# A whole-bank output norm in a hand-written order, other boundaries, and another spread of the conditioning products

## The chip, the cores and the metric

The kernel runs on one core of one Trainium2 chip. The metric is the time of one execution on the device, in microseconds. A core has a matrix engine (PE; its weight loads, PEld, run beside its products), a vector engine (DVE), a scalar engine (ACT), POOL, and SP, which here only issues loads. PE writes into PSUM banks of 128 x 512 floats, which DVE and ACT read.

## The reference

Two layers of a decoder trunk over 256 tokens of width 1024. Each layer has three sublayers, a half-step SwiGLU, a mixer and another half-step SwiGLU: six in all, named ffn0, hg, ffn1, ffn2, gm, ffn3 here. Each sublayer normalises before and after, and takes a shift, a scale and a gate from a vector c:

```python
def sublayer(x, fn, pre_g, post_g, shift, scale, gate, res_w):
    h = rms_norm(x, pre_g) * (1.0 + scale) + shift
    return x + res_w * gate * rms_norm(fn(h), post_g)
...
mod = (cond @ ada_w[i] + ada_b[i])
```

The first mixer is HGRN2, a gated linear recurrence of 8 heads, whose output is normalised per head and token over 128 values, multiplied by a silu gate, and projected:

```python
o = rms_norm(o, out_norm) * gate
return o.reshape(B, S, D_MODEL).astype(h.dtype) @ w_out
```

The second mixer is a gMLP: gelu, a layer norm of one half, a causal mixing over tokens, a product with the other half, a projection.

## The kernel before, in words

The 256 tokens are two tiles (t = 0, 1) of 128. x stays in SBUF through all six sublayers, so time goes from sublayer to sublayer and all else is prefetched.

**Weights.** They come in blocks of two halves. For a half, `cast` (L113) has SP load 512 KB into a buffer `raw` and ACT round it to the high part (L122); `sub` (L129) has DVE take the low part, raw minus high (L132). `halves(n)` does both for n halves. A product of activations and weights is three matmuls, high x high, high x low, low x high (`mm3`, L162 to L164). `next_block` hands out a block that is ready and prepares some ahead.

**Conditioning products.** `cond @ ada_w` is cut into 144 products over a 128 x 1024 tile, each a 512 KB load (`ada`) by SP and one DVE instruction with its reading of the sum (L192). Some are made when shift and scale of the next sublayer (`pre_cols`) or the gate (`gate_tile`) need them; the others are spread between the weight blocks: `pace(upto, blocks)` (L154) says that by the end of so many blocks the products up to `upto` are to be made. The table `bgs` in `run` gives `upto` for each sublayer. The load goes on the same SP queue as the weights, and its tile must have been freed by DVE.

**Order.** A scheduler places most instructions; the order that the program is written in counts there, with a few added "after" edges (`self.gate`, `self.hold`). From `boundary` (L297) to `close` (L371) the order of ACT, DVE and PE is as written: a `manual_schedule` region.

**A boundary**, between two sublayers, computes the last output matmuls `mm(t, h)` for each tile and each half h of 512 columns; squares the halves (ACT, `square`, L235); multiplies by the gate (DVE, `gated`, L310); scales the sum and adds it to x in two halves (`residual`, L255); squares x; scales it to `xn` (`scaled`, L293 DVE and L295 ACT); transposes it on PE into `npa` (L271); and makes the next sublayer's input, its high part on ACT (`h_high`, L274), then a full copy `hf` on DVE (L284) and the low part on DVE (L287), both in `h_low`. `half_mean` (L242) makes the bias `be` of the second half's sqrt. In between stands `p0`, the first matmuls of the next sublayer over t = 0 (`pps`, L412): 30 of them, then npa of (1,0), 6, npa of (1,1), and the rest. `halves(4)` and `halves(2)` at the start, one half block around the second residual, and one before `p0`, keep the weights coming: 8 in all.

**The HGRN** (`hgrn`, L627) makes its projections in `feat` and `tok`, and its attention in `attn(hb)` for two blocks of four heads. `attn` goes through seven levels of chunk size h (64, 32, 16, 8, 4, 2, 1): DVE makes differences and products (L724, L729, L735), ACT an exponential (L80), PE scores into `ab` (L741), DVE copies them under a mask (L712). Each level is a chain DVE, ACT, DVE, PE, DVE. `zip_steps` deals one step of projection to each step of attention, so that PE has work: attn(0) is mixed with `feat` and `tok`, attn(1) with the last `tok` and with `outs`, which holds the norm of the first four heads and their 48 output matmuls. At the end PE forms the outputs of four heads in two PSUM banks, `ops` (L774, L776).

`finish(hb, ops)` (L781) is the output norm. ACT squares each of the eight 128 x 128 pieces with an accumulated sum (L787); `r8` is the inverse root of the mean, for hb = 0 by Newton steps on DVE (`rsqrt`, L84 to L101), for hb = 1 by ACT's sqrt and a reciprocal (L792); DVE multiplies each piece by r8 and the gate `gg` in one instruction out of PSUM (L800); PE transposes four of them into a bank `ots` (L805); ACT and DVE split that into high and low part (L809, L810), the stationary operands of the output product.

**The gMLP** (`gmlp`, L912) first makes six column blocks of v with their statistics (L924, L955), then calls `G_fn` (the gate of its own end, with the conditioning products that this needs, and a transpose `gps`, L219), loads the token mixing weights and three small tables (`gbinu`, `glng`, `glnb`), and then goes through twelve units u.

Of the kernel before, what the change touches and what calls it, by code (L numbers as in the profile page):

```python
# [18 lines left out]
P = 128  # L19
# [14 lines left out]
class Body:  # L34
# [216 lines left out]
    def residual(self, t, yg, r, st=None):  # L251

        for h in range(2):
            hs = slice(512 * h, 512 * h + 512)
            self.nc.vector.scalar_tensor_tensor(self.x[t][:, hs], yg[:, hs], r, self.x[t][:, hs],  # L255
                                                op0=ALU.mult, op1=ALU.add)
# [21 lines left out]
    def h_low(self, t, h, pa, cols):  # L278
        nc = self.nc
        A, sh = cols  # L280
        hf = self.scr.tile([P, 512], F32, tag="hf", name="hf")
        for k in range(4):
            kc, ks = 4 * h + k, slice(k * P, (k + 1) * P)
            nc.vector.tensor_scalar(hf[:, ks], pa[:, ks], A[:, kc:kc + 1], sh[:, kc:kc + 1],  # L284
                                    op0=ALU.mult, op1=ALU.add)
        hs4 = slice(4 * h, 4 * h + 4)
        return nc.vector.tensor_sub(self.h2[:, 1, t, hs4, :], hf.rearrange("p (k t) -> p k t", k=4),  # L287
                                    self.h2[:, 0, t, hs4, :])
# [7 lines left out]

    def boundary(self, y, G, mm, cols, table):  # L297


        nc = self.nc  # L300
        E = mybir.EngineType
        self.region = self.tc.manual_schedule(engines={E.Activation, E.DVE, E.PE})
        self.region.__enter__()
# [12 lines left out]
        self.halves(4)  # L316
# [5 lines left out]
        self.halves(2)  # L322
# [3 lines left out]
        r = self.inv_rms(sy)  # L326
        self.residual(0, yg, r, sx)
        r = self.inv_rms(sx)
# [22 lines left out]
        self.cast()  # L351
        self.residual(1, yg1, r, sx1)
        self.sub()
# [10 lines left out]
        do(p0[36:])  # L364
        self.h_low(1, 0, pa0, cols)
        dve = self.h_low(1, 1, pa1, cols)
# [260 lines left out]
    def hgrn(self, hT, G_fn, pre_next, nxt, bg):  # L627
        nc, tc = self.nc, self.tc
        self.pace(bg, 9)
# [63 lines left out]
        def attn(hb, bank, res):  # L693
# [73 lines left out]
            for u in range(2):  # L767
                ops = bank().rearrange("p (t h v) -> p t h v", t=NT, h=2)
                for t in range(NT):
                    for hd in range(2):  # L770
                        hl = 2 * u + hd
                        c0 = (4 * hb + hl) * P
                        if t == 1:
                            nc.tensor.matmul(ops[:, t, hd, :], S10[:, hl * P:(hl + 1) * P], v[:, 0, c0:c0 + P],  # L774
                                             start=True, stop=False)
                        nc.tensor.matmul(ops[:, t, hd, :], St[:, hl * S + t * P:hl * S + (t + 1) * P],  # L776
                                         v[:, t, c0:c0 + P], start=t == 0, stop=True)
                res.append(ops)
            yield

        def finish(hb, ops, sqrt=False):  # L781
            ss = self.tiny.tile([P, 8], F32, tag="ss8", name="ss8")
            o4 = [o.rearrange("p t h v -> p (t h) v") for o in ops]
            for u in range(2):
                for i in range(4):
                    junk = self.scr.tile([P, 512], BF16, tag="junka", name="junka")
                    nc.scalar.activation(junk[:, 0:P], o4[u][:, i, :], AF.Square, accum_out=ss[:, 4 * u + i:4 * u + i + 1])  # L787
            nc.vector.tensor_scalar(ss, ss, 1.0 / P, EPS, op0=ALU.mult, op1=ALU.add)
            r = self.tiny.tile([P, 8], F32, tag="r8", name="r8")
            if sqrt:  # L790
                self.tact(ss, ss, AF.Sqrt)
                nc.vector.reciprocal(r, ss)  # L792
            else:
                self.rsqrt(r, ss)
            for u in range(2):
                pair = 2 * hb + u
                on = self.t2().rearrange("p (i v) -> p i v", i=4)
                for i in range(4):
                    t, c0 = i // 2, (2 * pair + i % 2) * P
                    nc.vector.scalar_tensor_tensor(on[:, i, :], o4[u][:, i, :], r[:, 4 * u + i:4 * u + i + 1],  # L800
                                                   gg[:, t, c0:c0 + P], op0=ALU.mult, op1=ALU.mult)
                ps = self.acc.tile([P, 512], F32, tag="acc", name="ots")
                for i in range(4):
                    c0 = (i % 2) * S + (i // 2) * P
                    nc.tensor.transpose(ps[:, c0:c0 + P], on[:, i, :], self.ident)  # L805
                if not oall:
                    oall.extend([self.wtile() for _ in range(2)])
                oT = [o[:, 512 * pair:512 * pair + 512] for o in oall]
                nc.scalar.activation(oT[0], ps, AF.Copy, scale=self.onorm)  # L809
                nc.vector.scalar_tensor_tensor(oT[1], ps, self.onorm, oT[0], op0=ALU.mult, op1=ALU.subtract)  # L810
                oTs.append([o.rearrange("p (h s) -> p h s", h=2) for o in oT])
# [68 lines left out]
        self.ahead = 1  # L880
        oall = []
        y = None

        def outs():
            finish(0, ops[0])
            yield
            y = self.y_banks()
            state["y"] = y
            for i in range(2):
                wo = nb()  # L890
                for k in range(2):
                    for t in range(NT):
                        for h in range(2):
                            self.out_mm(y[t][h], t, h, oTs[i], k, wo, k, i + k == 0, False)
                    yield

        zip_steps(attn(1, bank_a, ops[1]), [
            tok(lambda t, ps: nc.scalar.copy(gg[:, t, 512:], ps)), outs()], 0)
        y = state["y"]
# [4 lines left out]
        finish(1, ops[1], True)  # L904
# [3 lines left out]

# [3 lines left out]
    def gmlp(self, hT, G_fn, pre_next, nxt, bg):  # L912
# [43 lines left out]
        G = G_fn()  # L956
# [7 lines left out]
        bcol = self._load("gbinu", [P, 24])  # L964
        gcol = self._load("glng", [P, 24])
        lcol = self._load("glnb", [P, 24])
# [21 lines left out]
        for u in range(12):  # L988
# [89 lines left out]
    def late_consts(self):  # L1078
# [4 lines left out]
        self.onorm = self._load("onorm", [P, 1])  # L1083

# [15 lines left out]
    def run(self):  # L1100
# [10 lines left out]
        bgs = {"ffn0": 46, "hg": 64, "ffn1": 92, "ffn2": 118, "gm": 138, "ffn3": 144}  # L1111
        for s, kind in enumerate(subs):
# [10 lines left out]
            def nxt(y, G, mm, s=s, st=st):  # L1123
# [3 lines left out]
                else:  # L1127
                    self.boundary(y, G, mm, st["cols"], tables[subs[s + 1][0]])
# [112 lines left out]
```

## Time and profile before

| | us |
|---|---|
| median of three runs | 1200.78 |
| lowest and highest | 1199.64, 1204.22 |
| the profiled execution, its own time | 1199.71 |
| its span | 1197.9 |
| busy in it: PE, DVE, ACT | 1144.4, 909.9, 663.3 |

The mean granted clock of PE over the span is 0.982. By the npa transposes the boundaries lie at about 213 us (ffn0 to hg), 397 to 411 (to ffn1), 588 to 601 (to ffn2), 787 (to gm) and 1013 us (to ffn3). In the rows that follow, an entry is start, duration, engine, line, operation, output <- input and, in square brackets, how long the engine had stood idle before it and what ended that. A group of instructions has xcount, then busy us and mean ns, then the idle time before them with its releasers.

### The profile page before, as it was taken

The numbers are of one execution on the slowest core, as the hardware profiler recorded it, in microseconds if no ns is written. First come the engines' busy times: TensorE is split into PE (matmuls) and PEld (weight loads), VectorE is DVE, ScalarE is ACT, GpSimd is POOL, SyncE is SP. The second block draws the span as 40 slices with busy tenths as digits, with TensorE's granted clock in tenths as the row PEclk, the third lists the DMA queues.
The fourth block names the chain that finished last, engine by engine and source line by source line (L and its number), as shares of the span: only waits on it lengthen the run. The fifth ranks groups of instructions, "written<-read, shape, count | busy, mean of one in ns | idle before, by whom it ended". The sixth has DMA issues, their size and how long they took to land.

```text
span 1197.9 us, 17119 instructions
## 1 busy us (share of the span) xinstructions
PE 1144.4 (96%) x6518; PEld 997.4 (83%) x6518; DVE 909.9 (76%) x1391; ACT 663.3 (55%) x1054; POOL 6.8 (1%) x16
## 2 busy tenths in 40 slices
PE   7999998898798899999999999999999999999997
PEld 6989997798787688888788888877798997888886
DVE  6987786779867789985589986476898777866642
ACT  6454446668547755555565555553664456645531
POOL 0000000000000000000000000000000000000000
PEclk9999999898899999999999999999999999999999
DMA  9889898296305389986279996426687764766630
GB/s 349 311 315 331 320 351 287 95 327 233 125 35 193 106 293 365 333 307 224 94 261 339 344 334 227 165 80 222 234 316 276 265 201 131 247 216 226 207 106 36
DMA packets 79764, 282.31 MB, mean 236 GB/s; under 512 B 9873, under 2 KB 10561, under 8 KB 79682
## 3 DMA queue, kind: packets, MB, share of 16 engines
q1 hardware_dynamic: 78626, 278.05, 66.0%
q0 software_dynamic: 1056, 3.17, 0.8%
q8 instruction: 51, 0.84, 0.3%
q14 instruction: 31, 0.25, 0.1%
HBM read 280.11 MB, written 1.07 MB: 235 GB/s over the span
## 4 chain that ended last, share of the span: by engine, by line
PE 83%; DVE 8%; DMA 4%; ACT 4%; issue 1%; SPq 0%; DVEq 0%; ACTq 0%
PE ups L437 17%; PE ups L438 9%; PE y L162 8%; PE y L163 8%; PE y L164 8%; PE pps L412 7%; PE ups L557 4%; PE ups L445 4%; PE ups L443 4%; PE ups L444 4%; DVE w L132 2%; PE ab L741 2%; DMA raw<-in_wffn 2%; ACT w L122 1%; PE vps L1003 1%
## 5 line engine op out<-in xcount | busy, mean ns | idle before, releaser
L132 DVE TENSOR_TENSOR w<-raw,w 128x1024 fp32r<-128x1024 f32 x376 | 453.8, 1223 | 113.5 <-ACT w L122 105.5
L122 ACT CAST w<-raw 128x1024 fp32r<-128x1024 f32 x376 | 387.1, 1050 | 167.7 <-DMA raw<-in_wffn 66.0
L437 PE MATMUL ups<-h,w 128*128 128x512 f32 x864 | 302.0, 393 | 0.0
L438 PE MATMUL ups<-h,w 128*128 128x256 f32 x864 | 242.0, 280 | 0.0
L437 PEld LDWEIGHTS ups<-h,w 128*128 128x128 f32 x864 | 161.7, 187 | 36.4
L192 DVE CUSTOM_DVE_ANT_0 ada<-ada,cond 128x1024 f32<-128x1024 f32 x144 | 173.6, 1221 | 21.7 <-DMA ada<-in_ada 21.7
L162 PE MATMUL y<-w,t 128*128 128x512 f32 x448 | 179.7, 402 | 0.0
L163 PE MATMUL y<-w,t 128*128 128x512 f32 x448 | 178.2, 398 | 0.3 <-DVE w L132 0.3
L164 PE MATMUL y<-w,t 128*128 128x512 f32 x448 | 177.7, 397 | 0.0
L438 PEld LDWEIGHTS ups<-h,w 128*128 128x128 f32 x864 | 163.3, 189 | 1.0
L445 PE MATMUL ups<-h,w 128*128 128x256 f32 x416 | 117.9, 283 | 2.1 <-DVE rs_sd L89 1.2
L443 PE MATMUL ups<-h,w 128*128 128x256 f32 x416 | 118.3, 284 | 0.0
L444 PE MATMUL ups<-h,w 128*128 128x256 f32 x416 | 117.7, 283 | 0.0
L412 PE MATMUL pps<-w,h 128*128 128x512 f32 x480 | 115.1, 396 | 0.2 <-DVE h L287 0.2
L412 PEld LDWEIGHTS pps<-w,h 128*128 128x128 f32 x480 | 89.9, 190 | 19.2 <-DVE h L287 0.6
L164 PEld LDWEIGHTS y<-w,t 128*128 128x128 f32 x448 | 84.6, 189 | 20.3
L162 PEld LDWEIGHTS y<-w,t 128*128 128x128 f32 x448 | 84.7, 189 | 18.9
L163 PEld LDWEIGHTS y<-w,t 128*128 128x128 f32 x448 | 84.7, 189 | 18.9 <-DVE w L132 1.4
L445 PEld LDWEIGHTS ups<-h,w 128*128 128x128 f32 x416 | 79.7, 191 | 2.5 <-DVE w L132 2.5
L443 PEld LDWEIGHTS ups<-h,w 128*128 128x128 f32 x416 | 79.7, 192 | 1.0 <-issue 0.2
L444 PEld LDWEIGHTS ups<-h,w 128*128 128x128 f32 x416 | 79.7, 192 | 0.8 <-issue 0.2
L80 ACT ACTIVATE t<-t 128x256 f32<-128x256 f32 (+2 forms) x70 | 36.6, 524 | 50.4 <-DVE t L490 41.7
(196 smaller groups left out, 1327.1 us busy)
## 6 DMA issues: line engine op xcount, KB each, us to landing
raw<-in_wffn SPq DMA_DIRECT2D x264, 512.0 KB, 5.5
ada<-in_ada SPq DMA_DIRECT2D x144, 512.0 KB, 6.7
raw<-in_wgmu SPq DMA_DIRECT2D x48, 512.0 KB, 5.0
raw<-in_whg SPq DMA_DIRECT2D x40, 512.0 KB, 5.2
raw<-in_wgmv SPq DMA_DIRECT2D x24, 512.0 KB, 5.0
G<-gflat POOLq DMA_DIRECT2D x6, 512.0 KB, 5.1
t<-in_gbin SPq DMA_DIRECT2D x6, 256.0 KB, 5.6
x<-in_x SPq DMA_DIRECT2D x2, 512.0 KB, 4.3
```

The lines of the kernel that those rows point to most:

```text
L122: self.after(self.nc.scalar.copy(hi[:, sl], raw), self.hold[0])
L132: self.after(self.nc.vector.tensor_sub(lo[:, sl], raw, hi[:, sl]), self.hold[1])
L162: self.paced(mm(ps, l[0], r[0], start=start, stop=False))
L163: mm(ps, l[0], r[1], start=False, stop=False)
L164: mm(ps, l[1], r[0], start=False, stop=stop)
L192: self.after(nc.vector.tensor_tensor_reduce(t, t, self.cond, 1.0, 0.0, ALU.mult, ALU.add, self.mod[i // 24][:, i % 24:i % 24 + 1]), self.h ...
L412: lambda g=g, i=i, j=j, kc=kc, w=w: mm(res[g][t], h2[:, i, t, kc, :], w, start=kc + i + j == 0, stop=i == 1 and kc == KC - 1)))
L437: self.paced(mm(ps, u[0], self.h2[:, :, :, kc, :], start=kc == 0, stop=False))
L438: self.last = mm(ps[:, 1, :], u[1], self.h2[:, 0, :, kc, :], start=False, stop=kc == KC - 1)
L443: self.paced(mm(o, u[0], h[0], start=start, stop=False))
L444: mm(o, u[0], h[1], start=False, stop=False)
L445: self.last = mm(o, u[1], h[0], start=False, stop=stop)
```

## The change

Five edits.

1. `finish` becomes `stats`, `turn` and `split`. ACT squares a whole bank at a time (two instructions), DVE sums the squares (two `reduce_sum`), multiplies whole banks by the gate (two `tensor_mul`), and multiplies the eight pieces by r8 in SBUF. The norm of the second four heads is now in the hand-written region, and 24 of the 48 output matmuls of the first four heads (`products(1)`) no longer stand in attn(1): 15 of them come before the first transposes of the second norm, 3 between, 6 behind.
2. `boundary`: `half_mean` comes after both halves of the residual; `h_low` is split into `h_full` (the full copy) and `h_low` (the subtraction). For (0,1) the full copy is on ACT and the subtraction on DVE behind the second residual. `p0` is divided 35, 6 and the rest. One half block goes to the end. A `plan` says how many halves stand at four places: 4, 2, 0, 0, and at the HGRN's end 2, 1, 1, 1.
3. The spread of the conditioning products: 40 by the end of ffn0 where it was 46, so that the HGRN makes 24 and not 18, over 14 blocks and not 9; 120 by the end of ffn2 where it was 118.
4. In the gMLP `G_fn` moves from before the layer norm's statistics to behind unit 8.
5. The three small tables of the gMLP are loaded with the other late constants, during ffn0.

```diff
-                if h == 0:
-                    self.half_mean(st)
+        if st is not None:
+            self.half_mean(st)
...
-        self.halves(4)
+        self.halves(plan[0])
...
-        self.halves(2)
+        self.halves(plan[1])
...
+        for _ in range(plan[2]):
+            self.cast()
         self.residual(0, yg, r, sx)
+        for _ in range(plan[2]):
+            self.sub()
...
-        self.h_low(0, 0, pa0, cols)
-        self.h_low(0, 1, pa1, cols)
-        w = [[self.ready.pop(0) for _ in range(2)] for _ in range(2)]
-        self.res, go = self.proj(w)
+        self.h_low(0, 0, self.h_full(0, pa0, cols))
         sq(1, 1, sy1)
         gated(1, 1, yg1)
         r = self.inv_rms(sy1)
-        self.cast()
+        for _ in range(plan[3]):
+            self.cast()
+        hf = self.h_full(1, pa1, cols, scalar=True)
         self.residual(1, yg1, r, sx1)
-        self.sub()
+        for _ in range(plan[3]):
+            self.sub()
+        self.h_low(0, 1, hf)
...
-        do(p0[0:30])
+        do(p0[0:35])
         pa0, _ = self.h_high(1, 0, xn, cols)
-        do(p0[30:36])
+        do(p0[35:41])
         pa1, act = self.h_high(1, 1, xn, cols)
...
+        self.halves(1)
...
-        self.pace(bg, 9)
+        self.pace(bg, 14)
...
+        def stats(hb, ops, sqrt):
+
+            ss = self.tiny.tile([P, 8], F32, tag="ss8", name="ss8")
+            r = self.tiny.tile([P, 8], F32, tag="r8", name="r8")
+            og, sqs = self.t4(), []
+            for u in range(2):
+                sqs.append(self.t2().rearrange("p (i v) -> p i v", i=4))
+                nc.scalar.activation(sqs[u], ops[u].rearrange("p t h v -> p (t h) v"), AF.Square)
+
+            def gated(u):
+                c0 = 2 * (2 * hb + u) * P
+                nc.vector.tensor_mul(og[:, 512 * u:512 * u + 512].rearrange("p (t c) -> p t c", t=NT),
+                                     ops[u].rearrange("p t h v -> p t (h v)"), gg[:, :, c0:c0 + 2 * P])
+
+            for u in range(2):
+                nc.vector.reduce_sum(ss[:, 4 * u:4 * u + 4], sqs[u], axis=mybir.AxisListType.X)
+                if u == 0:
+                    gated(0)
...
+            if sqrt:
+                self.tact(ss, ss, AF.Sqrt)
+                self.cast()
+                gated(1)
+                nc.vector.reciprocal(r, ss)
...
+            for i in range(4):
+                nc.vector.tensor_scalar(on[:, i, :], on[:, i, :], r[:, 4 * u + i:4 * u + i + 1], None, op0=ALU.mult)
...
+        fill = products(1)
...
+        self.open()
+        self.gate = state["ops"]
+        for op in fill[:5]:
+            op()
+        og, r = stats(1, ops[1], True)
+        ps = [turn(1, 0, og, r)]
+        fill[5]()
+        ps.append(turn(1, 1, og, r))
+        self.sub()
+        for op in fill[6:]:
+            op()
+        for u in range(2):
+            split(1, u, ps[u])
...
-        G = G_fn()
...
+            if u == 8:
+                G = G_fn()
...
-        bgs = {"ffn0": 46, "hg": 64, "ffn1": 92, "ffn2": 118, "gm": 138, "ffn3": 144}
+        bgs = {"ffn0": 40, "hg": 64, "ffn1": 92, "ffn2": 120, "gm": 138, "ffn3": 144}
```

A `fill` entry is three matmuls. Line numbers shift with the change: in the kernel after it L741 is L758, L724 and L729 are L741 and L746, L735 is L752, L712 is L729, L805 is L836, L810 is L845.

What DVE does at the first output norm, in attn(1), from the second Newton step to the eight products by r8. Before:

```order
375 L98 TENSOR_TENSOR rs_q<-rs_y 128x8
376 L99 TENSOR_TENSOR rs_q<-rs_q,rs_hv 128x8
377 L101 SCALAR_TENSOR_TENSOR rs_y<-rs_q,rs_y 128x8
378 L98 TENSOR_TENSOR rs_q<-rs_y 128x8
379 L99 TENSOR_TENSOR rs_q<-rs_q,rs_hv 128x8
380 L101 SCALAR_TENSOR_TENSOR r_3474<-rs_q,rs_y 128x8
381 L800 SCALAR_TENSOR_TENSOR t_3495<-ab,r_3474,w 128x128 x2
382 L712 COPY_PREDICATED t_3290<-lmask,ab 128x32x16
```

And in the changed kernel:

```order
371 L101 SCALAR_TENSOR_TENSOR rs_y<-rs_q,rs_y 128x8
372 L192 ISA ada,mod_108<-ada,cond 128x1024
373 L192 ISA mod_108 128x1
374 L98 TENSOR_TENSOR rs_q<-rs_y 128x8
375 L752 TENSOR_TENSOR t_3553<-t_3553,w 128x256x2
376 L99 TENSOR_TENSOR rs_q<-rs_q,rs_hv 128x8
377 L192 ISA ada,mod_108<-ada,cond 128x1024
378 L192 ISA mod_108 128x1
379 L101 SCALAR_TENSOR_TENSOR r_3451<-rs_q,rs_y 128x8
380 L206 TENSOR_TENSOR shift<-mod_108,adab 128x8
381 L207 TENSOR_TENSOR A<-mod_108,adab 128x8
382 L832 TENSOR_SCALAR t_3452<-t_3452,r_3451 128x128 x8
```

Two conditioning products, the shift and the scale of the next sublayer, and a product of the attention's next but one level now stand between the Newton steps and the products by r8; two more conditioning products stand a few rows further up.

DVE at the second output norm, before:

```order
399 L132 TENSOR_TENSOR w<-raw,w 128x1024 x5
400 L788 TENSOR_SCALAR ss_3660<-ss_3660 128x8
401 L132 TENSOR_TENSOR w<-raw,w 128x1024
402 L792 RECIPROCAL r_3678<-ss_3660 128x8
403 L800 SCALAR_TENSOR_TENSOR t_3681<-ab,r_3678,w 128x128 x4
404 L800 SCALAR_TENSOR_TENSOR t_3693<-ab,r_3678,w 128x128 x4
```

And in the changed kernel:

```order
395 L814 TENSOR_REDUCE ss_3670<-t_3673 128x4
396 L810 TENSOR_TENSOR t_3672<-ab,w 128x512
397 L132 TENSOR_TENSOR w<-raw,w 128x1024 x2
398 L814 TENSOR_REDUCE ss_3670<-t_3675 128x4
399 L817 TENSOR_SCALAR ss_3670<-ss_3670 128x8
400 L810 TENSOR_TENSOR t_3672<-ab,w 128x512
401 L822 RECIPROCAL r_3671<-ss_3670 128x8
402 L832 TENSOR_SCALAR t_3672<-t_3672,r_3671 128x128 x8
```

No weight subtraction stands between the sum and the reciprocal any more; two stand between the two reductions.

DVE at the boundary behind the HGRN, from the gate product of (1,0) to the second residual, before:

```order
420 L310 TENSOR_TENSOR yg<-y_3538,G 128x512
421 L284 TENSOR_SCALAR hf<-npa,A,shift 128x128 x4
422 L287 TENSOR_TENSOR h_3836<-hf,h_3836 128x512
423 L284 TENSOR_SCALAR hf<-npa,A,shift 128x128 x4
424 L287 TENSOR_TENSOR h_3836<-hf,h_3836 128x512
```

And in the changed kernel, where L319, L287 and L293 are what L310, L284 and L287 were:

```order
417 L319 TENSOR_TENSOR yg<-y_3523,G 128x512
418 L287 TENSOR_SCALAR hf<-npa,A,shift 128x128 x4
419 L293 TENSOR_TENSOR h_3820<-hf,h_3820 128x512
420 L319 TENSOR_TENSOR yg<-y_3524,G 128x512
421 L248 RECIPROCAL r<-sq 128x1
422 L255 SCALAR_TENSOR_TENSOR x_103<-yg,r,x_103 128x512 x2
423 L242 TENSOR_SCALAR be<-s_3809 128x1
424 L132 TENSOR_TENSOR w<-raw,w 128x1024
425 L293 TENSOR_TENSOR h_3820<-hf,h_3820 128x512
```

The subtraction for (0,1) has moved from row 424 before to the last row here, behind the residual, the bias and a weight subtraction.

More of the change, by code (lines that the diff above doesn't have):

```diff
@@ L303, in boundary @@
         self.region.__enter__()
+    def boundary(self, y, G, mm, cols, table, plan=(4, 2, 0, 0)):
+        nc = self.nc
         sq = lambda t, h, st: self.square(y[t][h], st[0], h)
@@ L350, in boundary @@
         r = self.inv_rms(sy1)
-        self.cast()
+        for _ in range(plan[3]):
+            self.cast()
+        hf = self.h_full(1, pa1, cols, scalar=True)
         self.residual(1, yg1, r, sx1)
-        self.sub()
+        for _ in range(plan[3]):
+            self.sub()
+        self.h_low(0, 1, hf)
+        w = [[self.ready.pop(0) for _ in range(2)] for _ in range(2)]
+        self.res, go = self.proj(w)
         r = self.inv_rms(sx1)
@@ L775, in attn @@
                                              start=True, stop=False)
[L776 to L777 removed]
+                        state["ops"] = nc.tensor.matmul(
+                            ops[:, t, hd, :], St[:, hl * S + t * P:hl * S + (t + 1) * P],
+                            v[:, t, c0:c0 + P], start=t == 0, stop=True)
                 res.append(ops)
@@ L788, in finish @@
             nc.vector.tensor_scalar(ss, ss, 1.0 / P, EPS, op0=ALU.mult, op1=ALU.add)
-            r = self.tiny.tile([P, 8], F32, tag="r8", name="r8")
             if sqrt:
                 self.tact(ss, ss, AF.Sqrt)
+                self.cast()
+                gated(1)
                 nc.vector.reciprocal(r, ss)
             else:
+                gated(1)
                 self.rsqrt(r, ss)
[L795 to L811, printed above, removed]
@@ new lines, in stats, with turn @@
+            return og, r
+        def turn(hb, u, og, r):
+            on = og[:, 512 * u:512 * u + 512].rearrange("p (i v) -> p i v", i=4)
+            for i in range(4):
+                nc.vector.tensor_scalar(on[:, i, :], on[:, i, :], r[:, 4 * u + i:4 * u + i + 1], None, op0=ALU.mult)
+            ps = self.acc.tile([P, 512], F32, tag="acc", name="ots")
+            for i in range(4):
+                c0 = (i % 2) * S + (i // 2) * P
+                nc.tensor.transpose(ps[:, c0:c0 + P], on[:, i, :], self.ident)
+            return ps
@@ L813, in hgrn, with split @@
+        def split(hb, u, ps):
+            pair = 2 * hb + u
+            if not oall:
+                oall.extend([self.wtile() for _ in range(2)])
+            oT = [o[:, 512 * pair:512 * pair + 512] for o in oall]
+            nc.scalar.activation(oT[0], ps, AF.Copy, scale=self.onorm)
+            nc.vector.scalar_tensor_tensor(oT[1], ps, self.onorm, oT[0], op0=ALU.mult, op1=ALU.subtract)
+            oTs.append([o.rearrange("p (h s) -> p h s", h=2) for o in oT])
         ybank = {"i": 0}
@@ L879, in hgrn, with products @@
         G = G_fn()
-        self.ahead = 1
         oall = []
-        y = None
+        def products(i):
+            wo = nb()
+            return [lambda k=k, t=t, h=h: self.out_mm(y[t][h], t, h, oTs[i], k, wo, k, i + k == 0, False)
+                    for k in range(2) for t in range(NT) for h in range(2)]
         def outs():
-            finish(0, ops[0])
+            og, r = stats(0, ops[0], False)
+            for u in range(2):
+                split(0, u, turn(0, u, og, r))
             yield
[L887 to L894, printed above, removed]
+            y.extend(self.y_banks())
+            for j, op in enumerate(products(0)):
+                op()
+                if j == 3:
                     yield
+            yield
+        y = []
         zip_steps(attn(1, bank_a, ops[1]), [
             tok(lambda t, ps: nc.scalar.copy(gg[:, t, 512:], ps)), outs()], 0)
-        y = state["y"]
         self.table("silu_and_others")
@@ L903, in hgrn @@
         self.table("sqrt_and_others")
-        finish(1, ops[1], True)
+        self.ahead = 0
+        fill = products(1)
         wos = [nb()]
@@ L1083, in late_consts @@
         self.onorm = self._load("onorm", [P, 1])
+        self.gm_cols = [self._load(n, [P, 24]) for n in ("gbinu", "glng", "glnb")]
     def first_h(self, kc):
```

36 lines of the change are left out of this document (18 added, 18 removed).

## The prediction

> **What bounds the kernel now.** I read the page first, then the waits of PE, then windows of 40 us, then the timelines of the stretches in which PE loses time. The page has the busy shares of the engines and, further down, the share of each engine in the chain that ended last:
>
> ```profile
> PE 1144.4 (96%) x6518; PEld 997.4 (83%) x6518; DVE 909.9 (76%) x1391; ACT 663.3 (55%) x1054; POOL 6.8 (1%) x16
> PE 83%; DVE 8%; DMA 4%; ACT 4%; issue 1%; SPq 0%; DVEq 0%; ACTq 0%
> ```
>
> PE is the bound nearly everywhere, and the change leaves its matmuls as they are. So it can gain only what PE loses: the waits, and the time in which PE's clock is halved after them. The waits of PE (total, times, longest):
>
> ```profile
> PE npa L271 <- DVE be L242: 9.7, 2, 8.1
> PE npa L271 <- DVE xn L293: 7.5, 4, 2.4
> PE ab L741 <- DVE t L735: 6.6, 1, 6.6
> PE ab L741 <- ACT L L679: 5.1, 1, 5.1
> PE ots L805 <- DVE t L800: 5.0, 1, 5.0
> PE gps L219 <- DVE w L924: 1.1, 1, 1.1
> ```
>
> These 35.0 us are all at places that the change touches: the five places where one sublayer ends and the next begins (npa), two in the HGRN attention (ab), its last norm (ots), and the normalisation of the gMLP. Windows show where PE's loss is concentrated; columns are busy time of PE, PEld, DVE, ACT, POOL, then the granted clock, DMA share and GB/s:
>
> ```profile
> 160.00:200.00 40.00, 40.00 (x252) 36.00 (x252) 29.45 (x34) 20.37 (x23) 0.56 (x1) 1.00 0.91 321
> 200.00:240.00 40.00, 31.91 (x137) 25.97 (x136) 30.31 (x58) 25.49 (x51) 0.00 (x0) 0.87 0.42 139
> 240.00:280.00 40.00, 40.00 (x328) 39.68 (x327) 33.78 (x54) 28.11 (x44) 0.00 (x0) 1.00 0.79 287
> 280.00:320.00 40.00, 28.26 (x172) 26.88 (x172) 35.30 (x59) 29.55 (x53) 0.00 (x0) 0.76 0.52 181
> 320.00:360.00 40.00, 39.60 (x265) 35.92 (x264) 28.15 (x59) 17.95 (x44) 1.08 (x2) 0.98 0.20 67
> 360.00:400.00 40.00, 33.48 (x175) 27.71 (x175) 29.82 (x45) 28.98 (x57) 0.00 (x0) 0.96 0.55 184
> 205.00:210.00 5.00, 0.41 (x2) 0.00 (x0) 3.87 (x5) 2.63 (x5) 0.00 (x0) 0.88 0.89 297
> 210.00:215.00 5.00, 1.49 (x6) 1.40 (x7) 2.12 (x6) 3.27 (x9) 0.00 (x0) 0.50 0.61 220
> 215.00:220.00 5.00, 5.00 (x17) 3.98 (x16) 3.62 (x10) 3.33 (x10) 0.00 (x0) 0.60 0.02 5
> 220.00:225.00 5.00, 5.00 (x23) 4.13 (x22) 4.04 (x8) 3.08 (x9) 0.00 (x0) 1.00 0.01 2
> 840.00:845.00 5.00, 5.00 (x17) 3.95 (x16) 5.00 (x7) 1.92 (x4) 0.52 (x1) 0.66 0.77 248
> ```
>
> A share of 0.88, then 0.50, then 0.60, if the clock is either half or full, is half clock for 1.2 + 5 + 4 = 10.2 us around the 8.1 us wait; 0.66 behind the gMLP's short waits is half clock for 3.4 us. [...]
>
> **The change part by part.** The sum is made against the profiled execution, 1199.71 us, whose span is 1197.9; it lies 1.1 us under the median 1200.78, within the runs' 1199.64 to 1204.22.
>
> *First boundary (ffn0 to HGRN).* ACT's stream there (start, duration):
>
> ```profile
> 202.04 0.59 ACT L235 ACTIVATE junka<-y 128x512 bf16<-128x512 f32 x1
> 204.65 1.05 ACT L122 CAST w<-raw 128x1024 fp32r<-128x1024 f32 x1 [1.93 <-DMA raw<-in_whg]
> 206.22 1.05 ACT L122 CAST w<-raw 128x1024 fp32r<-128x1024 f32 x1 [0.52 <-DMA raw<-in_whg]
> 207.17 0.59 ACT L235 ACTIVATE junka<-y 128x512 bf16<-128x512 f32 x1
> L192 DVE CUSTOM_DVE_ANT_0 ada<-ada,cond 128x1024 f32<-128x1024 f32 x144 | 173.6, 1221 | 21.7 <-DMA ada<-in_ada 21.7
> ada<-in_ada SPq DMA_DIRECT2D x144, 512.0 KB, 6.7
> ```
>
> The square of the second output half stands behind casts whose weights come late, and the whole norm, and then npa on PE, behind that square. The sublayer's DMA runs at 0.91 and 321 GB/s. Six conditioning products less take 6 x 0.512 MiB = 3.1 MB from it, 3.1 MB / 321 GB/s = 9.8 us of transfers, and 6 x 1.22 = 7.3 us from DVE. Casts up to 9.8 us earlier are more than the 5 us by which the square waits (202.04 to 207.17). So I take the 8.1 us wait as gone to some 0.5, and with it half of the 1.2 + 4 us of half clock in which PE has work (17 matmuls in 215 to 220 against 23 in the next 5 us, 6 x 5/23 = 1.3 us, and about 0.6 before 215): 7.6 + 1.9 = -9.5. Bounds: -10 if the wait goes wholly, -3 if only a third of the transfer time reaches the casts. What is late next is the chain square, sqrt, scale itself, 1 to 2 us.
>
> *The HGRN's middle.* The six products are now made there (24 in 14 blocks, not 18 in 9), and by the order of DVE the attention has one more before its first norm: 7 x 1.22 = 8.5 us more on DVE before that norm's transposes. The first norm's own cost, from rows of 270 to 400 and of a boundary:
>
> ```profile
> L800 DVE SCALAR_TENSOR_TENSOR t<-ab,r,w 128x128 f32<-128x128 f32 x16 | 4.4, 345 | 0.1
> L787 ACT ACTIVATE junka<-ab 128x128 bf16<-128x128 f32 x16 | 4.4, 277 | 3.7 <-PE ab L776 3.3
> L787 ACT ACTIVATION_READ_ACCUMULATOR junka<-ab 128x1 f32 x16 | 3.1, 196 | 0.0
> L310 DVE TENSOR_TENSOR yg<-y,G 128x512 f32<-128x512 f32 x3 | 2.0, 683 | 0.0
> L293 DVE TENSOR_SCALAR xn<-x,r 128x512 f32<-128x512 f32 x2 | 1.0, 487 | 0.1
> ```
>
> Removed per norm: 8 squares with their reads on ACT, (4.4 + 3.1) / 2 = 3.75 us, and 8 products on DVE, 2.2 us. Added: two whole-bank squares, 0.59 each as the one at 202.04, 1.2 us on ACT; on DVE two gate products as L310, 1.37, eight 128 x 128 products out of SBUF, between a quarter of L293 (0.12) and L800's mean (0.34) each, 1.0 to 2.8, I take 0.2 and so 1.6; two reductions that the trace does not show, between nothing and L310's 0.68 twice, 0 to 1.4, and I take the upper end since each reads a full bank's worth of elements. DVE pays 4.4 - 2.2 = 2.2 us more, ACT 2.5 less. [...]
>
> So DVE has 8.5 + 2.2 = 10.7 us more before the first norm's transposes. From 240 to 360 it is busy 33.78 + 35.30 + 28.15 = 97.2 of 120, and PE waits there only at the two ab places. The waits of 5.1 and 6.6 us and their half clock (0.76 of 280 to 320) are for DVE and ACT chains, which the new order partly puts ahead; but what PE gains there it waits again at the transposes, which need DVE to have done everything ahead of them. If DVE kept all its idle 22.8 us less 10.7, PE would gain 12; with its idle only half usable (11.4), it loses nothing and gains nothing. My walk through DVE's new order reaches the transposes about when before does, with PE some 9 us early. I take +1.5 for the half clock that follows; bounds -12 and +5.
>
> *The last norm.* Before:
>
> ```profile
> 379.56 1.05 ACT L122 CAST w<-raw 128x1024 fp32r<-128x1024 f32 x1 [1.28 <-DMA raw<-in_wffn]
> 382.01 2.16 DVE L800 SCALAR_TENSOR_TENSOR t<-ab,r,w 128x128 f32<-128x128 f32 x8
> 382.51 1.93 PE L805 MATMUL ots<-ident,t 128*128 128x128 f32 x7 [4.95 <-DVE t L800]
> ```
>
> Now 15 matmuls stand ahead of the first transposes and 3 between (before 12 and none), each about 5/23 = 0.22 us: 0.7 us more cover on either side; the chain is 3.75 - 1.2 = 2.5 us shorter on ACT; the first transposes need four small products (0.8 us) and not the eight of 2.16, 1.4 less; of the reductions and gate products (2.7 us) the first pair runs beside the second square, 1.4 more. That is 2.5 + 1.4 - 1.4 + 0.7 = 3.2. One cast still stands ahead of the sqrt. I take -3, bounds -5 and 0. The 24 matmuls are no new work: they are taken from the second attention, where they filled its waits, which the bound of +5 above holds.
>
> *HGRN to ffn1.* Here lies the longest of the four waits for xn:
>
> ```profile
> 409.07 0.66 PE L271 MATMUL npa<-ident,xn 128*128 128x128 f32 x4 [2.41 <-DVE xn L293]
> ```
>
> The casts are spread 2, 1, 1, 1, and the low half (0,1), whose subtraction of 0.69 us stood ahead of the second gate product, comes after the second residual and another block's subtraction: by my walk some 3.5 us after PE wants it, which takes the place of this wait of 2.4. The wait for the other npa of this boundary (9.7 - 8.1 = 1.6 in the row of be) falls by some 1, since the square no longer stands between the residual's halves. Sum 0, bounds -2 and +3.
>
> *The three other boundaries.* One of them:
>
> ```profile
> 594.45 0.75 DVE L255 SCALAR_TENSOR_TENSOR x<-yg,r,x 128x512 f32<-128x512 f32 x1
> 596.00 0.15 DVE L242 TENSOR_SCALAR be<-s 128x1 f32<-128x1 f32 x1 [0.79 <-ACT junka L235]
> 598.80 0.66 PE L271 MATMUL npa<-ident,xn 128*128 128x128 f32 x4 [1.57 <-DVE xn L293]
> ```
>
> The second residual half no longer waits for the square of the first (0.79); four full copies of 128 x 128 move to ACT; the low subtraction no longer precedes the gate product, and PE has 35 matmuls ahead of npa, not 30 (5 x 0.22 = 1.1 us). Each of these is about as large as the wait of 1.6. Of the 7.5 us of the row of xn 2.4 is HGRN to ffn1 and 5.1 these three. I take -5, bounds -5.6 (with what each loses at its restart) and -3.
>
> *gMLP.* Two products of the next gate, the first at 834.61 and waiting 4.81 us for its load, stand ahead of what PE waits for:
>
> ```profile
> 834.61 1.23 DVE L192 CUSTOM_DVE_ANT_0 ada<-ada,cond 128x1024 f32<-128x1024 f32 x1 [4.81 <-DMA ada<-in_ada]
> 838.93 0.50 PE L163 MATMUL pps<-w,h 128*128 128x512 f32 x1 [0.86 <-DVE w L132]
> ```
>
> They move behind u == 8, and the three small loads to the start. PE's waits are 1.1 + 0.9 us with an estimated 0.4 of restart, and the half clock takes 17 matmuls where 23 would be: 1.3. I take -3.7; bounds 0 (the weights are late for another reason) and -5.
>
> Sum: -9.5 + 1.5 - 3 + 0 - 5 - 3.7 = -19.7; 1199.7 - 19.7 = 1180.
>
> **The rivals.** *DVE becomes the bound of the second attention.* Place: the first norm's transposes. DVE's idle is used less than by half, PE waits 12 to 15 us there, at half clock after it: +10 on the sum, 1190. For it: DVE's 35.30 of 40 at 280 to 320. Against: DMA at 0.20 and DVE at 28.15 in 320 to 360.
> *The pacing does not help* (the change doesn't do there what it says): DMA stays full since the weights ahead take what is freed, the casts are as late as before, and the 9.5 stay: 1189.5. For it: 0.91 and 0.89 up to the end of the stretch.
> *Better:* DVE packs its work, the HGRN gains 12: about 1167.
> *Slower.* SP, one queue, stands before conditioning loads until DVE has freed a tile:
>
> ```profile
> 208.93 24.97 SPq L57 DMA_DIRECT2D ada<-in_ada  x2
> ```
>
> Weights behind such a load come late. With 24 products in the HGRN instead of 18, DVE behind its plan holds SP, SP holds the weights of w_out and of ffn1, and PE waits for both. It costs what SP stands beyond the slack of the weights; to end above 1206 it has to eat the 19.7 and 6 more, 26 us, one such stop of 25 wholly on PE's path: 1207. Against it: the stop shown cost PE nothing; all that PE loses in 200 to 240 (40 - 31.91 = 8.1) lies in 205 to 215 (4.59 + 3.51), before its end.
>
> **How the numbers follow.** Measurements of this kernel can tell about 0.5%, 6 us, from no change. The forecast has 0.53 (1173 to 1187), DVE as the bound 0.17, no help from the pacing 0.08, the better case 0.11, slower 0.05, and a mixture of losses that leaves the time within 6 us of before 0.06. The range of 8 in 10 goes from 1164 to 1193. Faster by over 0.5% are the forecast, the better case and nearly all of the two rivals near 1190: 0.85; within 0.5% 0.09; slower 0.06.
>
> **What would show it.** Right: PE's npa wait at about 205 under 1 us with no half clock; casts there not waiting for DMA; the waits of PE moved from ab to ots of the first norm; npa at the other boundaries under 0.5; no wait at gps. Wrong: raw<-in_whg still ahead of the square at the first boundary; PE at ots over 12 us, with DVE fully busy before it; a time above 1194.

## The result and the profile after

The changed kernel takes 1181.74 us (median of 4 runs, 1177.77 to 1184.81) where the one before takes 1202.49 (1199.64 to 1204.22): a ratio of 0.9837, 95% interval 0.9813 to 0.986. On a second chip it gave 1182.55 (1178.80 to 1185.73) against 1199.39: a ratio of 0.9861 (0.9839 to 0.9884), 16.8 us less. The profiled execution has a span of 1183.0 us against 1197.9. PE's waits in it (total, times, longest), to be held against those of before:

```profile
PE ots L836 <- DVE t L832: 10.2, 2, 8.8
PE vps L1050 <- DVE t L1057: 5.1, 4, 1.8
PE pps L429 <- DVE h L293: 3.1, 1, 3.1
PE npa L271 <- DVE be L242: 3.0, 2, 2.7
PE ab L758 <- ACT t L80: 2.7, 1, 2.7
PE ab L793 <- DVE t L729: 1.4, 1, 1.4
PE ab L758 <- DVE t L752: 0.2, 1, 0.2
```

The four waits for xn (7.5) and the one at gps are gone; npa for be has gone from 9.7 to 3.0; the two waits at the scores, 11.7, are 2.9. In their place stands 8.8 us at the first transposes, 3.1 behind the HGRN, and a wait that did not exist before, 5.1 us at vps, the PSUM tile of the token mixing product in the gMLP's units. The windows (PE, PEld, DVE, ACT, POOL, then PE's clock, DMA share, GB/s):

```profile
200.00:240.00 40.00, 37.35 (x186) 31.46 (x185) 29.28 (x53) 25.25 (x53) 0.00 (x0) 0.96 0.40 131
240.00:280.00 40.00, 37.30 (x311) 37.10 (x311) 36.40 (x62) 33.06 (x54) 0.00 (x0) 0.99 0.93 336
280.00:320.00 40.00, 39.89 (x261) 36.59 (x262) 38.12 (x61) 28.17 (x53) 1.08 (x2) 0.93 0.42 135
320.00:360.00 40.00, 30.98 (x183) 27.73 (x182) 33.87 (x71) 20.76 (x29) 0.00 (x0) 0.83 0.44 145
205.00:210.00 5.00, 2.49 (x9) 2.10 (x10) 2.02 (x6) 4.20 (x12) 0.00 (x0) 0.73 0.63 226
210.00:215.00 5.00, 5.00 (x23) 4.22 (x22) 3.99 (x9) 4.33 (x13) 0.00 (x0) 0.92 0.02 5
340.00:345.00 5.00, 0.00 (x0) 0.00 (x0) 5.00 (x15) 1.06 (x1) 0.00 (x0) 0.55 0.66 211
345.00:350.00 5.00, 3.37 (x17) 3.30 (x17) 4.46 (x17) 2.25 (x4) 0.00 (x0) 0.50 0.86 306
350.00:355.00 5.00, 5.00 (x19) 4.35 (x19) 3.96 (x5) 4.95 (x5) 0.00 (x0) 0.59 0.52 146
```

From 240 to 360 PE is busy 37.30 + 39.89 + 30.98 = 108.2 of 120, where before it was 40.00 + 28.26 + 39.60 = 107.9: the HGRN gained next to nothing, its wait has only moved. DVE is busy there 108.4 where it was 97.2. What DVE did while PE stood still:

```profile
337.77 1.22 DVE L192 CUSTOM_DVE_ANT_0 ada<-ada,cond 128x1024 f32<-128x1024 f32 x1
340.35 1.22 DVE L192 CUSTOM_DVE_ANT_0 ada<-ada,cond 128x1024 f32<-128x1024 f32 x1
342.93 1.22 DVE L192 CUSTOM_DVE_ANT_0 ada<-ada,cond 128x1024 f32<-128x1024 f32 x1
344.83 1.22 DVE L192 CUSTOM_DVE_ANT_0 ada<-ada,cond 128x1024 f32<-128x1024 f32 x1
346.20 1.65 DVE L832 TENSOR_SCALAR t<-t,r 128x128 f32<-128x128 f32 x8
```

Four conditioning products stand between the Newton steps, and the eight products that PE waits for begin behind the last. Between the lines shown DVE also makes five instructions of the attention, 0.7 us each.

### The profile page after: what moved, and what is told of

Its sections match the earlier page's. It is cut to its first block, busy times and chain, and to the rows that moved or that the text cites. A ratio compares the mean times of both kernels' runs of the same rounds, so it can differ in the third digit from the quotient of the medians.

```text
span 1183.0 us, 17089 instructions
## 1 busy us (share of the span) xinstructions
PE 1141.4 (96%) x6518; PEld 995.8 (84%) x6518; DVE 904.7 (76%) x1379; ACT 666.3 (56%) x1046; POOL 6.8 (1%) x16
## 3 DMA queue, kind: packets, MB, share of 16 engines
HBM read 280.11 MB, written 1.07 MB: 238 GB/s over the span
## 4 chain that ended last, share of the span: by engine, by line
PE 84%; DMA 5%; DVE 5%; ACT 3%; issue 1%; SPq 0%; DVEq 0%; ACTq 0%
PE ups L454 17%; PE pps L429 9%; PE ups L455 9%; PE y L163 8%; PE y L164 8%; PE y L162 8%; PE ups L574 4%; PE ups L462 3%; PE ups L460 3%; PE ups L461 3%; DMA ada<-in_ada 2%; PE ab L758 2%; DVE w L132 2%; DMA raw<-in_wgmu 2%; ACT w L122 1%
```

## The experiments

Each ran beside the kernel before on its chip; ratios are to that. Line numbers shift from kernel to kernel, tile names do not. A stretch is timed in the traces from the first npa transpose of one boundary to that of the next.

**The spread taken back, in the changed kernel:**

```diff
-        self.pace(bg, 14)
+        self.pace(bg, 9)
...
-        bgs = {"ffn0": 40, ...
+        bgs = {"ffn0": 46, ...
```

> The changed kernel with the old spread of the conditioning products (46 by the end of ffn0; the HGRN makes 18 over 9 blocks). Theory A: the new spread buys the first boundary (PE loses 6.5 us less there by the two traces) and pays for it in the HGRN, where six products of 1.22 us stand on DVE ahead of the first norm's transposes. Then the npa wait at 205 comes back to about 8 us with 10 us of half clock, PE's wait at ots of the first norm falls from 8.8 to 0 to 2 us, and the time stays within 4 us of the changed kernel's 1181.7. Theory B: the spread is a plain gain (the HGRN's wait has other causes): ots stays at 7 to 9 us, and the time is 6 us or more above the changed kernel's.

Measured: 1181.15, ratio 0.9849 (0.9836 to 0.9863): no change. Its waits:

```profile
PE npa L271 <- DVE be L242: 7.4, 2, 7.0
PE ots L836 <- DVE t L832: 2.3, 2, 1.2
```

Theory A: 4.3 us more at the boundary, and at the first transposes 8.84 - 1.07 = 7.8 less (the 1.2 in the row is the second norm's). New waits for weights at fps, a projection of the HGRN (2.3 + 1.4, near 281 us), and more half clock at that place (13.6 us from 280 to 300, where the changed kernel has 6.9 from 275 to 290) take a part of that back. PE reaches the npa at the HGRN's end at 386.50, in the changed kernel at 386.72: in the new order the spread is a trade, one for one.

**The spread alone, in the kernel before** (the same two lines, the other way).

> The kernel before with only the new spread (40 by the end of ffn0, HGRN 24 over 14 blocks). Theory A: the npa wait of 8.1 at 205 falls to 2 to 3 us, and the HGRN, whose old order waits at the scores, loses 5 to 8 us more there or at the transposes: 1198 to 1205. Theory B: the boundary's gain is kept: 1193 to 1196.

Measured: 1194.72, ratio 0.9961 (0.9948 to 0.9975), 4.8 us under the 1199.47 of before there.

```profile
PE ots L805 <- DVE t L800: 10.8, 2, 5.8
PE npa L271 <- DVE be L242: 5.3, 2, 3.7
PE ab L741 <- DVE t L735: 3.9, 1, 3.9
PE ab L741 <- ACT t L80: 2.0, 1, 2.0
```

The time is theory B's. The boundary's 8.1 became 3.7, near what A had; but A's further loss in the HGRN did not come: waits at the scores fell by 11.7 - 5.9 = 5.8 us, just what came in at the first transposes (5.8). So with the old order the spread was a gain, with the new order it was not; the two edits overlap. Theory A holds for the place of the cost, not for its size in the old order.

**The gMLP's gate call moved back** (the call from behind unit 8 to before the statistics), run twice.

> The changed kernel with the gMLP's gate call back before the layer norm (the small tables still loaded early). Theory A: the move gained nothing on balance, because DVE still stands before conditioning products whose loads are late, only later, in the units: PE waits at vps fall from 5.1 to 1 to 2 us, a wait of 1 to 2 us at the gate's transpose or behind it comes back, time within 2.5 us of the changed kernel. Theory B: the vps waits are of the units' own making, and the move is worth its 3.7 us: time 1185 to 1186, vps still at 4 to 5.

> The changed kernel with the gMLP's gate call back before the layer norm, a second time, since its one profile so far (1180.1) was faster than its other five times (1184.9 to 1189.1) and so does not show where they lose. Theory A: its losses lie in the gMLP, at vps and at late weights there, 4 to 6 us more than in the changed kernel, so that a profile near 1186 shows PE losing 14 us or more from 800 to 1000. Theory B: it is no slower than the changed kernel on the same chip (ratio within 0.002).

Measured: 1186.12, ratio 0.9886 (0.9867 to 0.9906), and 1184.99, 0.9881 (0.9864 to 0.9899), the second beside the changed kernel's own 0.9861 (0.9839 to 0.9884): these two overlap (the first run's lies above the first result's, from another chip), so that by the times the move is worth some 2 us, or a little more, or nothing. In the first run the time and vps (5.0) are about as theory B said; in the second PE loses 7.1 us from 800 to 1000 and not the 14 of theory A. But no theory had the main thing: the wait at the gate's transpose did not come back with the call. That transpose in the second run has no wait, and PE loses its time in the units, as in the changed kernel:

```profile
833.25 0.27 PE L219 MATMUL gps<-ident,gate 128*8 128x128 f32 x1
PE vps L1051 <- DVE t L1058: 7.1, 5, 3.1
```

The two conditioning products that stood ahead of it belong to the gate, products 119 and 120; with 120 made by the end of ffn2, not 118, the call finds them done. So the spread's second number is enough to take the wait away. Whether the place of the call would have been enough with 118 was not run. The place is not without use, though: from the boundary before the gMLP to the one behind it PE takes 225.8 us in the kernel before, 224.2 and 225.3 with the call back, and 219.1 to 223.6 (median 221.9) in the nine traces that have 120 and the call behind unit 8. As far as so few traces tell, the call behind unit 8 is worth some 3 us, and with the call back the waits at vps eat what the wait at the transpose gave.

**The low part of (0,1) ahead of the second residual:**

```diff
+        self.h_low(0, 1, hf)
         self.residual(1, yg1, r, sx1)
         for _ in range(plan[3]):
             self.sub()
-        self.h_low(0, 1, hf)
```

> The changed kernel with the low part of (0,1) ahead of the second residual at all boundaries. Theory A: the wait of 3.1 us at pps behind the HGRN is that subtraction standing behind the residual and a weight subtraction: it goes to under 0.5, half clock after it (6.8 us) goes too, and the time falls 3 to 5 us; at the other boundaries the residual is 0.6 us later and npa of (1,0) waits at most 0.5 us each. Theory B: the subtraction waits for ACT's full copies, which stand behind a sqrt and a cast: then DVE stands there instead, the residual comes late, and the npa of (1,0) waits 2 to 3 us: time unchanged within 2 us.

Measured: 1175.79, ratio 0.9811 (0.9793 to 0.9829). The wait at pps falls from 3.1, not quite away:

```profile
PE pps L429 <- DVE h L293: 1.3, 1, 1.3
```

No half clock follows it, and no xn is waited for at any boundary. Theory A, with 1.3 us left; that DVE waits there for ACT's full copies is likely from the next two boundaries of this trace, where it stands 0.93 us for hf of L285 ahead of the same subtraction (at 576.55 and 762.94). By the ratios it is 3 to 6 us under the two results of the changed kernel, which ran on other chips (its interval is clear of the second and overlaps the first). The traces show it at the place: from this boundary to the next PE takes 186.6 us in all five kernels with this edit and the same plan of weight halves, and 188.4 to 191.1 in the six traces without it. The 1.8 of the wait is always gained, and up to 2.7 us on top when half clock follows the longer wait (6.8 us at half in the changed kernel's first trace, none in three others).

**The old output norm for the first four heads**, the new one for the last four (`outs` calls the old `finish(0, ...)`; all else as changed).

> The changed kernel with the old output norm (eight squares of 128 columns with accumulated sums on ACT, eight products out of PSUM by r8 and gate on DVE) for the first four heads only. Theory A (PE's 8.8 us at the transposes is DVE's total of work before them): DVE has about 2.2 us less, the wait falls by 1.5 to 3, and the time by 1 to 3 us. Theory B (ACT's squares are in the chain): the eight squares and reads cost 2.5 us more there, the wait stays or grows, time the same or up to 2 us longer.

Measured: 1176.63, ratio 0.9812 (0.9794 to 0.983), clear of the changed kernel on the same chip (0.9839 to 0.9884).

```profile
PE ots L823 <- DVE t L818: 7.0, 1, 7.0
```

The wait falls by 1.9, theory A's amount for 2.2 us less on DVE. (The scheduler also put one conditioning product, 1.2 us, behind the transposes and two attention instructions, 1.2 us, ahead of them; the two cancel.) The whole difference, 5.9 us by the medians, is more than that place shows. Of the 3.9 us between the two profiled executions 1.9 lie in the HGRN, 1.6 behind it, where the same wait of 3.1 us is followed by 3.4 us of half clock in one and by none in the other, and 1.8 in the gMLP; the first boundary and the last sublayer take 1.4 back. The edit touches only the first of these places. That the whole-bank norm costs about 2 us where DVE is the bound is shown; the rest is scatter as far as the traces tell.

**Seven conditioning products moved behind the first norm** on DVE, on top of the low part ahead:

```diff
+        self.limit = self.ada_next
         oall = []
...
                 split(0, u, turn(0, u, og, r))
+            self.pace(bg, 3)
+            self.ahold = self.norm
             yield
```

where `norm` is the last of the eight products by r8 and `ahold` an edge from it to each conditioning product until `pre_next` has returned.

> The changed kernel with the low part of (0,1) ahead of the second residual (as in the run before), and seven conditioning products of the second attention moved on DVE from before the eight products by r8 to behind them. Theory A (PE's wait at the first transposes is DVE's total before them): 7 x 1.22 = 8.5 us less stand before them, the wait of 8.8 falls to 0 to 2 us with its half clock, and most of it is kept: 1168 to 1172. Theory B (it only moves on): DVE owes the seven products before the second norm, and PE waits 6 us or more in all at the last scores, the outputs or the second transposes: within 2.5 us of the run without this edit (1175.8).

Measured: 1185.79, ratio 0.9882 (0.9862 to 0.9903), 10 us above the run without it, or 8.5 by the ratios, since they ran on two chips. Its waits of PE; SP's, from 340 to 362, and SP's issues; ACT:

```profile
PE y L162 <- ACT w L845: 12.4, 1, 12.4
PE ots L837 <- DVE t L833: 2.2, 2, 1.8
```

```profile
SPq L57 <- DVE mod L193: 39.3, 6, 24.7
```

```profile
343.36 16.84 SPq L57 DMA_DIRECT2D ada<-in_ada  x6
360.30 1.98 SPq L57 DMA_DIRECT2D raw<-in_whg  x4
```

```profile
367.06 1.05 ACT L122 CAST w<-raw 128x1024 fp32r<-128x1024 f32 x1 [3.46 <-DMA raw<-in_whg]
379.52 1.26 ACT L845 ACTIVATE w<-ots,onorm 128x512 fp32r<-128x512 f32 x2
```

The first transposes now wait 1.8 us and no more: that the wait of 8.8 is DVE's work ahead of them is shown. But neither theory foresaw where it goes: SP spends 16.84 us on six conditioning loads, each of which waits for DVE to be done with an earlier product (24.7 us the longest), the weights behind them in its queue leave at 360.30 (342.21 in the run without this edit), and seven casts on ACT wait one after the other, four for these weights and three for the next, which leave from 369.39. The split of the second norm, behind those casts, reaches PE 12.4 us late. It is the mechanism of my rival on the slower side, at a third of the price that it would have needed.

**Four on one base.** The base has both edits that helped alone.

> The changed kernel with both edits that helped alone: the low part of (0,1) ahead of the second residual, and the old output norm for the first four heads. The two lie at different places (the boundary behind the HGRN, 390 us, and the first transposes, 337 us). If they add (3 to 4 and 5 to 6 us): ratio to the kernel before 0.975 to 0.979, 1170 to 1174. If the second only moves the time into a wait that the first already removed: 1175 to 1177.

> As c1, with 43 conditioning products by the end of ffn0 (HGRN 21) where c1 has 40 (24). Theory A (the spread trades the first boundary against the HGRN about one for one): the npa wait at 205 grows by 1 to 4 us, the wait at the first transposes (7.0) falls by about 3 x 1.22 = 3.7; time within 2 us of c1. Theory B: the first transposes' wait hangs on the order within attn(1) and not on the total: the wait stays, time 2 to 4 us above c1.

> As c1, with 126 conditioning products by the end of ffn2 where c1 has 120, so that gm makes 12 and not 18. Theory A (in the gMLP's units DVE stands before conditioning products whose loads are late, and PE waits for it at vps): waits at vps fall under 1 us in all, DVE waits less for ada, time 1 to 3 us under c1. Theory B (the units wait for late weights, and the products are not at fault): vps waits as in c1; or ffn2 pays for the six, and its end waits: time the same or longer.

> As c1, with the weight halves at the HGRN's boundary at 3, 2, 0, 0 where c1 has 2, 1, 1, 1. Theory A (spread casts keep ACT free for the squares): the squares stand behind casts that wait for DMA again, the npa wait of (0,0) there, 1.6 us before the change and 0.3 after, comes back, time 1 to 3 us above c1. Theory B: the plan is worth nothing, since the chain of residual and square is as long either way: within 1 us of c1.

| run | us | ratio | interval |
|---|---|---|---|
| c1, base | 1178.64 | 0.9821 | 0.9797 to 0.9845 |
| c2, 43 in ffn0 | 1179.97 | 0.9835 | 0.9818 to 0.9851 |
| c3, 126 by the end of ffn2 | 1172.72 | 0.9774 | 0.9757 to 0.9791 |
| c4, plan 3, 2, 0, 0 | 1173.95 | 0.9785 | 0.9765 to 0.9805 |

c1 was not the sum, though both places show their gain in its trace (ots 7.0, pps 1.3). Against the trace with the low part first alone, its first boundary waits 2.4 and not 1.4, with 3.4 us of half clock behind it where that one has none (granted from 200 to 240: 0.96 and 1.00), and its gMLP takes 2.4 us longer, with half clock once (0.96 from 880 to 920). Both places vary between traces of code that is the same there, so that scatter covers the sum. In the gMLP:

```profile
PE vps L1080 <- DVE t L1087: 3.4, 2, 2.2
DVE ada L192 <- DMA ada<-in_ada: 6.9, 5, 2.7
```

c3 takes six products out of the gMLP. PE waits only 0.2 us for DVE at vps, but 1.6 for ACT where c1 has 0.7, and DVE's own waits for conditioning loads from 785 to 985 fall:

```profile
PE vps L1080 <- ACT w L1078: 1.6, 1, 1.6
DVE ada L192 <- DMA ada<-in_ada: 5.0, 3, 2.6
```

The time fell as theory A said, and further (5.9 by the medians, the intervals apart); the waits at vps, 1.8 in all, stay above its 1 us. It has the lowest median here, 2.3% under the kernel before. That the six products are the cause is likely but not shown: 4.3 of the 5.1 us between the two traces lie in the gMLP's stretch, 223.6 us in c1 and 219.3 in c3, but two traces with 120 are as short there: 219.1 with the old first norm (vps 1.4 in all) and 219.9 in c4 (vps 2.3).

c2 is not A's trade: npa went from 2.4 to 5.0, but the first transposes only from 7.0 to 6.3, and the scores wait 2.9 more. At the HGRN's end PE is 3.4 us behind c1, so nothing of the boundary's loss came back there, as theory B had it; the time is nearer only because its gMLP took 1.5 less. The trade that held for six products from the changed kernel did not hold for three from c1.

For c4 the npa wait came back to 3.7 - 2.4 = 1.3, as A said, and pps fell from 1.3 to 0.3, so that at its place the plan is worth nothing, as B said. The 4.7 us by the medians are more than either allowed; in the traces they lie in the gMLP (3.7) and behind the first boundary, where c1 has those 3.4 us of half clock and c4 has none, and c4 changes neither. c3 and c4 together were not run.

## Why the prediction was right

It gave 1180 (1164 to 1193); 1181.74 was measured. That the two are so close is in part luck: nine executions of the changed kernel range over 8 us, and the terms err in both that were traced, at 1184.81 and 1178.80. Times from one first npa of a boundary to the next, in us against the kernel before (15 us less in all in the first, 21 in the second):

| stretch | forecast | first trace | second chip |
|---|---|---|---|
| to the first boundary's npa | -7.6 | -6.0 | -5.7 |
| HGRN with its last norm, and the restart before it | -4.4 | -4.8 | -7.1 |
| its end, ffn1 | +1.0 | +1.3 | +0.2 |
| ffn1's end, ffn2 | -1.7 | -1.8 | -1.8 |
| ffn2's end, gMLP | -5.4 | -2.5 | -4.8 |
| gMLP's end, ffn3 | -1.7 | -1.2 | -1.7 |

The forecast column is the prediction's terms laid on these stretches: -9.5 is 7.6 of wait and 1.9 of restart, the three boundaries' -5 is shared equally, and the HGRN's end is -1 before its npa and +1 behind it. The terms one by one:

*First boundary*, -9.5. Mechanism right, the size too large. The wait fell from 8.1 to 2.7, PE's busy time in 200 to 240 rose by 37.35 - 31.91 = 5.4, and half clock fell from 10.2 us to 2 x 5 x (0.27 + 0.08) = 3.5. The mis-sized term is "8.1 to some 0.5": ACT's casts still waited for DMA ahead of the square, which the prediction had named as a sign of being wrong, and the second square came at 202.08, 5.1 us earlier than before, not the 9.8 that the freed transfers would have allowed:

```profile
201.12 1.05 ACT L122 CAST w<-raw 128x1024 fp32r<-128x1024 f32 x1 [0.71 <-DMA raw<-in_whg]
202.08 0.58 ACT L235 ACTIVATE junka<-y 128x512 bf16<-128x512 f32 x1
```

In the other runs of the new order with 40 by the end of ffn0 it lay between 1.4 and 3.5. The rival that the pacing does not help is out all the same: with 46 again the wait was 7.0.

*The HGRN's middle*, +1.5. Right in both: the score waits went, PE stood 8.8 us at the first transposes (the walk said 9), and the sum changed by 0.3 us of PE's busy time. One part of the working was off without harm: 24 conditioning products lie between the first boundary and these transposes and 18 did before, so six more and not seven. The eight small products took 1.65 us, near the 1.6 taken. The clock row says why it did not gain more: half from 340 to 355, 13.6 us by 0.55, 0.50 and 0.59.

*The last norm*, -3. The wait fell from 5.0 to 10.2 - 8.8 = 1.4: 3.6, but the output matmuls of the heads (L793) now wait 1.4, where they waited 0.4 before (L776). That the 24 matmuls taken from there are missing is a likely reason, not tested alone.

*HGRN to ffn1*, 0. The forecast of a wait of 3.5 us for the low part of (0,1) in place of 2.4 was measured as 3.1; the other npa wait fell from 1.56 to 0.35. What no term had is that half clock behind the 3.1 can be twice as long as behind the 2.4: 6.8 us in the first trace, 3.4 in the second as before.

*The three other boundaries*, -5. All three waits are gone. At ffn1's end xn is ready at 586.2 and PE asks for it at 588.75:

```profile
585.69 0.49 DVE L299 TENSOR_SCALAR xn<-x,r 128x512 f32<-128x512 f32 x1
588.75 0.60 PE L271 MATMUL npa<-ident,xn 128*128 128x128 f32 x4
```

There are 2.5 us to spare, so in this trace the five more matmuls ahead (1.1 us) were not needed for it.

*gMLP*, -3.7. This step failed. "They move behind u == 8" was said to remove the wait; it was gone with the call at its old place too, so the 120 is enough without the move. And the gain was not kept whole: in its place came waits of PE for DVE at vps, 5.1 us here and 1.2 to 7.1 in the other runs with 120, which the term had at nothing. Of the 3.7 some 0.5 are left in the first trace and 2.8 in the second, once the 2.0 that the boundary before it waited are taken off. The 0.4 us of restart in the term were the author's estimate, which no run shows: behind the wait of 0.86 us the first matmul took 0.50 us where the next took 0.40.

By the medians the change is 20.8 us, by the two profiled executions 1199.71 - 1184.81 = 14.9, since the one after was the longest of its four, and on the second chip 16.8. The first trace falls short of the forecast by 1.6 us at the first boundary and 2.9 in the gMLP's stretch. The second trace reaches the forecast although its first boundary is as short of it: its HGRN has no half clock after the first boundary, nor after the wait at the heads' outputs, where the first trace has 3.5 and 3.4 us, and its vps waits 2.1.

Two slips in its sums change nothing: a stop of 25 us on PE's path gives 1180 + 25 = 1205 and not 1207, and 512 KB are 0.5 MiB and not 0.512, though the 3.1 MB are right.

On the clock behind PE's waits: after the wait of 2.7 us half clock lasted 3.5 us; after the 8.8 us wait PE worked at half from 346.63 to about 354, 7.5 us (0.50 and 0.59 from 345 to 355). At 840 in the kernel before, 3.4 us of half clock followed waits of 1.15 and 0.86 us (0.66 from 840 to 845).

## What to carry to other kernels

An idle share on the engine that is not the bound told little here: DVE was idle 22.8 of the 120 us from 240 to 360 in the kernel before, and with more work laid there PE waited 8.8 us for it at the first transposes. So spread work over it only where its chain does not end in something that the bound waits for, and count what stands ahead of that instruction in order. A load that waits for a buffer held the whole queue behind it here (16.84 us of SP, and weights 18 us later), so an edge put on its consumer was also an edge on the weights. When several edits sit in one stretch, undo them one by one; here a number in a table was enough to take the wait in the gMLP away, which the prediction had put down to the call that was moved. And read a difference stretch by stretch: where it lies in a place that the edit does not touch, it is scatter until more traces say otherwise.

## What the runs showed of the hardware that was not expected

Half clock (granted 0.50) around PE's waits lasted 3.4 us (from 207.3 and 364.4), 6.8 (from 279.0 and 395.1) and 13.6 (from 340.5) in the changed kernel's first trace, and 3.4 (from 383.1, 410.4 and 840.5) and 10.2 (from 209.0, 287.5 and 311.4) in the one before; the length of the wait alone did not tell which. The wait behind the HGRN is 3.06 to 3.08 us in six traces (two of the changed kernel, one with the spread back, two with the gate back, one with the old first norm); half clock after it lasted 6.8, 3.4, 0, 0, 6.8 and 0 us, and the same 15 matmuls behind it took 6.36, 5.30, 3.70, 3.71, 6.40 and 3.72 us. At the first boundary a wait of 2.65 us was followed by 3.4 us of it and one of 3.51 us, in the run with the old first norm, by none (granted 1.00 from 200 to 240). Nine executions of the changed kernel range from 1177.8 to 1185.7 us, and of the 6.0 us between the two that were traced 1.1 lie in this stretch. And kernels whose program is the same up to the first boundary waited there for 1.4 to 3.5 us in one execution or another.
